# Holding the weight sums and low parts of every seven-product block in program order on VectorE

## The chip, the cores and the metric

The kernel runs on one core of one Trainium2 chip. A core has five engines that run side by side, each through its own instructions in order, and wait for one another through semaphores: TensorE (PE in the profile, its weight loads PEld), VectorE (DVE), ScalarE (ACT), GpSimd (POOL) and SyncE (SP), which here issues the transfers of the weights. The metric is the time of one execution on the device in microseconds (us).

## The reference

One decoder layer on 256 positions of width 2048, in float32: a half-step SwiGLU feed-forward network (FFN) of width 5632, a mixer with two head groups that share one input projection (2048 by 5120) and one output projection (2048 by 2048), a second half-step FFN, and a last RMS norm.

```python
x = x + 0.5 * swiglu_ffn(rms_norm(x, g1), w_gate, w_up, w_down)
z = rms_norm(x, mix_norm) @ w_in               # lru_x, lru_gate, sc_b, sc_c, sc_x
y_lru = rg_lru(conv4(lru_x) + b, ...) * gelu(lru_gate)
y_sc = sc_b * conv3(sc_c * sc_x)
x = x + concat(rms_norm(y_lru), rms_norm(y_sc)) @ w_out
x = x + 0.5 * swiglu_ffn(rms_norm(x, g2), ...)
return rms_norm(x, final_norm)
# swiglu_ffn(x) = (silu(x @ w_gate) * (x @ w_up)) @ w_down
```

Nearly all the arithmetic is in the three matrix products of each FFN.

## The kernel before

**Units of weights.** Weights come in units of 512 by 512 numbers, 1 MB each, laid out as 128 partitions by 2048. A unit is loaded by SyncE into a `raw` buffer (`load`, L181). `parts_of` (L208) splits it: ScalarE rounds it into a high part `hi` in two halves (CAST, 128x1024), and VectorE subtracts (`lo = raw - hi`, 128x2048), so that the product keeps float32's precision. The rows of the data are split the same way. TensorE multiplies high by high, low data by high weights, and high data by low weights: for one block of 128 rows that is 8 matmuls on `hi` and then 4 on `lo`, each 128x512. There are two buffers for a pair `hi`, `lo` (`splits`), and inside an FFN and the second half of the output projection a third (`split_tiles`, L194, every third unit). Three `raw` buffers turn, and two more, of tag "kept", hold the units that a block adds up.

**Seven-product blocks.** `seven` (L411) multiplies two row blocks by a two-by-two square of weight units with seven products in place of eight (Strassen's scheme in Winograd's form), and adds the remaining two units of the inner dimension in the usual way (`usual`). I call the eleven steps of a block, in program order: p0 (unit w11), p4 (sum A = w12 - w11), x (unit b2, both row blocks), p5 (sum B = w22 - w11), x (b3), p6 (sum C = w22 - w12), p2 (w22), x (a2), p3 (sum D = w21 - w11), x (a3), p1 (w21). A p-step is 12 matmuls, an x-step 24. The four sums are VectorE instructions in place in the raw buffers of w11 and w12 (`raw<-raw,raw` in the profile); their casts and low parts follow. ScalarE copies finished products out of PSUM (`snap`: s1 and s5 after p0 and p4, u2 after p5, u3 after p6), and a callback adds them up: `done(1, 1)` after p6 takes u3, s5 and bank e; `done(0, 1)` after p2 takes bank c and u2; `done(1, 0)` after the last x takes bank a; `done(0, 0)` after p1 takes bank d and s1.

**Where the blocks stand.** Each FFN has a first stage of single products, then five pairs of blocks, `gate` and `up` (callbacks at L876 and L881): a gate block adds four times on VectorE and applies Silu on ScalarE; an up block adds and multiplies (eight small VectorE instructions) and its results are transposed on TensorE into `h` and split again (`settle`, L549). After pairs 0, 2 and 4 comes `down` (L790): an ordinary product for columns 0, a seven-product block (`d`) for columns 1 and 2, an ordinary product for columns 3. The mixer has one such block in the input projection (`sc_c`, L1139, tiles `in_c`) and one in the output projection (`o_q`, with callbacks `own` and `done`, L1286 to L1290). That makes 28 blocks: 20 gate and up, 6 down, 2 in the mixer.

**What sets the order.** Every instruction is recorded through a thin class `Engine` (all have line L43), and a list scheduler then places each engine's instructions by its own estimate of times, except those that are pinned. `keep_in_program_order` pins an instruction behind the instruction recorded just before it on the same engine. Before, `sp.held` pins the loads up to the first gate block, and the opening stage of the first FFN is pinned whole up to the middle of its first gate block; VectorE's work in the other blocks is free.

Of the kernel before, what the change touches and what calls it, by code (L numbers as in the profile page):

```python
# [13 lines left out]
ALU = mybir.AluOpType  # L14
# [35 lines left out]
def hybrid_block(ctx: ExitStack, tc: tile.TileContext, a: dict, out: bass.AP):  # L50
    nc = tc.nc
    Engine.pinned = False
    dve, act, pe, sp = (Engine(tc, e) for e in (nc.vector, nc.scalar, nc.tensor, nc.sync))
# [25 lines left out]
    bigs = ctx.enter_context(tc.tile_pool(name="bigs", bufs=10, side="left"))  # L79
# [92 lines left out]
    def big(name):  # L172

        return bigs.tile([P, UK, 2 * S], F32R, tag="big", name=name)
# [3 lines left out]
    extra = []  # L178
    turn_of = {"split": 0}

    def load(src, name, pieces=((0, UK),), loaded=None, kept=False):  # L181
        if kept and extra:
            raw = extra[0].tile([P, UK, CW], F32, tag="kept", name=f"raw_{name}", bufs=2)
        elif kept:
            raw = bigs.tile([P, UK, CW], F32, tag="big", name=f"raw_{name}")
        else:
            raw = raws.tile([P, UK, CW], F32, tag="raw", name=f"raw_{name}")
        for i, e in pieces:
            sp.dma_start(raw[:, i:e, :], src[i * P : e * P].rearrange("(j p) c -> p j c", p=P))
            if loaded:  # L190
                loaded(i)
        return raw

    def split_tiles(name):  # L194
        pool, bufs = splits, 2
        if extra:
            turn_of["split"] += 1
            if turn_of["split"] % 3 == 0:
                pool, bufs = extra[0], 1
        return [pool.tile([P, UK, CW], F32R, tag=part, name=f"{part}_{name}", bufs=bufs) for part in ("hi", "lo")]  # L200

# [209 lines left out]
    def seven(w, rows, cols, sf, xs, name, keep, done, between=None, early=False, own=None, factor=None):  # L411

        apart = {}
        if own:
            a, c = (bank(f"ps_{name}_{n}") for n in "ac")
            apart.update({(t, 1): bank(f"ps_{name}_x{t}1") for t in range(NT)})  # L420
            d, e = bank(f"ps_{name}_d"), None
            apart.update({(t, 0): bank(f"ps_{name}_x{t}0") for t in range(NT)})
        else:
            a, c, e, d = (bank(f"ps_{name}_{n}") for n in "aced")

        def get(u, n, kept=False):
            src = w[u * UK * P : (u + 1) * UK * P, cols[n] : cols[n] + CW]
            return load(src, f"{name}_{u}{n}", kept=kept)

        (r0, r1), two = rows, len(xs) > 1  # L430
        w11, w12 = get(r0, 0, True), get(r0, 1, True)
        b2, w22 = get(xs[0][0], 1), get(r1, 1)
        b3 = get(xs[1][0], 1) if two else None
        a2, w21 = get(xs[0][0], 0), get(r1, 0)
        a3 = get(xs[1][0], 0) if two else None

        def snap(ps, n):
            s = keep(f"{n}_{name}")
            if factor:
                act.activation(s, ps, AF.Copy, scale=factor[n])  # L440
            else:
                act.copy(s, ps)
            return s

        def product_of(i, raw, ps, begin=False, end=True, blk=None):
            multiply([(ps, sf[i], begin, end)], blk or parts_of(raw, f"{name}_p{i}"), True)

        def usual(i, raw, n, *targets, first=None):

            blk = first or parts_of(raw, f"{name}_x{i}{n}")  # L450
            if own:
                last = i == len(xs) - 1
                targets = [(apart[t, n], t, i == 0, last) for t in range(NT)]
            multiply([(ps, stationary(xs[i][1], t), b, z) for ps, t, b, z in targets], blk, True)
            if own and last:
                for t in range(NT):
                    own(t, n, apart[t, n])

        product_of(0, w11, a, True)
        dve.tensor_tensor(w11, w12, w11, op=ALU.subtract)  # L460
        if early:
            between("first sum")
        product_of(4, w11, c, True)
        blk = None
        if early:
            between("second product")
            hi, lo = split_tiles(f"{name}_x01")
            act.copy(hi, b2)
            s1 = snap(a, "s1")
            dve.tensor_tensor(w11, w22, w11, op=ALU.subtract)  # L470
            low_part(b2, hi, lo)
            blk = blocks(hi, lo)
        else:
            s1 = snap(a, "s1")
        s5 = snap(c, "s5")
        if between:
            between(0)
        usual(0, b2, 1, (e, 1, True, not two), (c, 0, False, False), first=blk)
        if between:
            between(1)  # L480
        if not early:
            dve.tensor_tensor(w11, w22, w11, op=ALU.subtract)
        if between:
            between("sum")
        product_of(5, w11, a)
        blk = blk2 = None
        if early:
            blk = parts_of(b3, f"{name}_x11")
            hi2, lo2 = split_tiles(f"{name}_p2")
            act.copy(hi2, w22)  # L490
            blk2 = blocks(hi2, lo2)
        u2 = snap(a, "u2")
        if between:
            between(2)
        if two:
            usual(1, b3, 1, (e, 1, False, True), (c, 0, False, False), first=blk)
        if early:
            between("third sum")
        dve.tensor_tensor(w12, w22, w12, op=ALU.subtract)
        if early:  # L500
            low_part(w22, hi2, lo2)
            between("third low")
        product_of(6, w12, a)
        u3 = snap(a, "u3")
        if early:
            between("fifth product")
        done(1, 1, e, [u3, s5])
        product_of(2, w22, c, blk=blk2)
        done(0, 1, c, [u2])
        usual(0, a2, 0, (d, 0, True, False), (a, 1, False, False))  # L510
        dve.tensor_tensor(w11, w21, w11, op=ALU.subtract)
        product_of(3, w11, a, end=own is not None or not two)
        if early:
            between("sixth product")
        if two:
            usual(1, a3, 0, (a, 1, False, True), (d, 0, False, False))
        done(1, 0, a, [])
        product_of(1, w21, d, own is not None)
        done(0, 0, d, [s1])

    def ffn(tag, norm, after, opening=False):
        with tc.tile_pool(name=f"ffn{tag}", bufs=1, side="left") as fp:
# [26 lines left out]
            def settle():  # L549
                while waiting:  # L550
                    turn_hidden(*waiting.pop(0))
# [88 lines left out]
            ps = {(m, t): bank(f"ps_{m}{tag}_0_{t}") for m in "gu" for t in range(NT)}  # L640
# [223 lines left out]
            for s in range(5):  # L864
                cs = (CW + 2 * s * CW, 2 * CW + 2 * s * CW)
# [21 lines left out]
                def meanwhile(i):  # L887
# [23 lines left out]
                sp.held = False  # L911
                seven(
                    wu, (0, 1), cs, sf, xs, f"u{tag}_{s}", keep, up,
                    (lambda i: settle() if i == 1 else None) if opening and s == 0 else None,
                )
                if s % 2 == 0:
                    down(s == 4)
# [49 lines left out]
    with tc.tile_pool(name="mixer", bufs=1, side="left") as mp, tc.tile_pool(name="mixw", bufs=2, side="left") as mw:  # L967
# [168 lines left out]
            last()  # L1136
            part(2)

        def sc_c():  # L1139
            r2 = work.tile([P, NT], F32, tag="r2", name="r2")  # L1140
            dve.tensor_tensor(r2, nm.r, nm.r, op=ALU.mult)
            rt = [r2[:, t : t + 1] for t in range(NT)]
# [18 lines left out]
            def done(t, n, ps, tiles):  # L1161
# [10 lines left out]
                    turn(1)  # L1172

            c0 = 3 * (D // 2)
            seven(
                w_in, (0, 1), (c0 + CW, c0), si, [(u, nm.xT[u]) for u in (2, 3)], "in_c", lambda name: free.pop(0), done,
                factor={"s1": rt[0], "s5": rt[1], "u2": rt[0], "u3": rt[1]},
            )
            return lambda: turn(0)

        def sc_x(ps, half):
# [24 lines left out]
        behind = None  # L1206
        for i, (use, part, half) in enumerate(order):
            ps = columns(w_in, part * (D // 2) + half * CW, nm.xT, f"in_{part}_{half}", behind)
            behind = None
            if i == 0:  # L1210
                flush()
                nm.factor()
                nm.diagonals()
                nm.rows()
                bc = nm.bc
                use(ps, half)
                behind = sc_c()
                gate_weights("a", a["lru_w_a"][0])
                gate_weights("i", a["lru_w_i"][0])
                yT += [big(f"yT_{u}") for u in range(KD // UK)]  # L1220
            else:
                use(ps, half)
# [11 lines left out]
        for g in range(2):  # L1234
            if g == 1:
                flush()
            ps = product(w_out, 0, (2 * g, 2 * g + 1), yT.__getitem__, f"o0_{g}")
# [11 lines left out]
    with tc.tile_pool(name="outs", bufs=1, side="left") as op:  # L1249
# [36 lines left out]
        def done(t, n, ps, tiles):  # L1286
            add(2 - n, t, 0, *([] if ps is None else [ps]), *tiles)
            added(2 - n)
# [10 lines left out]

    fss = const.tile([P, NT, NC_D], F32, name="fss")  # L1300
    ov = out.rearrange("(t p) d -> p t d", p=P)

    def last(c, t):
        if c == 0 and t == 0:
# [10 lines left out]
            return work.tile([P, 1], F32, tag=tag, name=f"{tag}_{t}")  # L1315


        dve.scalar_tensor_tensor(xr, xr, -0.5, fin[:, cs], op0=ALU.mult, op1=ALU.mult)
        if c == NC_D - 2:
            pre = held[t] = single("pre")  # L1320
            dve.reduce_sum(pre, fss[:, t, : c + 1], axis=AX.X)
# [71 lines left out]
```

## Time and profile before

| what | value |
|---|---|
| median of 3 runs (lowest to highest) | 1729.67 us (1729.08 to 1730.92) |
| profiled execution, its own time | 1729.74 us |
| its span in the profile | 1728.0 us |
| TensorE busy | 1716.6 us, 99% |
| VectorE busy | 1509.8 us, 87% |
| ScalarE busy | 1077.7 us, 62% |
| granted TensorE clock | 0.999 |

The span is the time from the program's first to its last profiled instruction; 1.74 us of the execution's time lie around it. A busy TensorE is not a TensorE at its peak, since matmuls overlap: what counts is the distance from one matmul's start to the next's. In the rows of the timeline a group of equal instructions is one line, with its start, the time it covers, and in square brackets the idle time before it and who ended that.

### The profile page before, as it was taken

Reading aid. Unit: us, or ns where it says so; the run is one execution under the profiler, and the core shown is the slowest. Engines: PE = TensorE matmul, PEld = TensorE weight load, DVE = VectorE, ACT = ScalarE, POOL = GpSimd, SP = SyncE. Lnnn points to the kernel's source line nnn. Section 1 sums busy time; section 2 is a strip of 40 time slices with the busy share of each in tenths; the row PEclk is TensorE's granted clock in tenths of the full one; section 3 lists DMA queues with packets and bytes.
Section 4 is the critical chain, followed back from the end, with each engine's and each line's share of the span. In section 5 each row is a group of like instructions: output and inputs, shape, how many; then the busy total and the mean of one; then the engine's idle time right before and its main releaser. Section 6 shows DMA issues by size and latency. Waiting matters only on the chain.

```text
span 1728.0 us, 20332 instructions
## 1 busy us (share of the span) xinstructions
PE 1716.6 (99%) x7985; PEld 1433.5 (83%) x7985; DVE 1509.8 (87%) x1239; ACT 1077.7 (62%) x1406; POOL 7.0 (0%) x34
## 2 busy tenths in 40 slices
PE   9999999999999999999999999999999999999998
PEld 8888888888888888878888888888888888888886
DVE  7998989899789898787897989889899887899896
ACT  7666566656466666667966657656556664656654
POOL 0100000000000000000000000000000000000000
PEclk9999999999999999999999999999999999999999
DMA  8564565666466556555566574675665646555743
GB/s 300 191 237 141 208 228 186 206 230 219 156 211 204 202 178 219 171 169 197 172 195 203 188 243 144 199 240 187 212 210 195 218 147 219 195 195 195 257 156 122
DMA packets 174223, 343.22 MB, mean 199 GB/s; under 512 B 5684, under 2 KB 8624, under 8 KB 174000
## 3 DMA queue, kind: packets, MB, share of 16 engines
q1 hardware_dynamic: 173632, 340.81, 58.5%
q8 instruction: 62, 1.02, 0.2%
q10 hardware_dynamic: 176, 1.06, 0.2%
q14 instruction: 33, 0.27, 0.0%
q0 software_dynamic: 320, 0.07, 0.0%
HBM read 339.82 MB, written 2.10 MB: 198 GB/s over the span
## 4 chain that ended last, share of the span: by engine, by line
PE 97%; DVE 1%; DMA 1%; issue 0%; ACT 0%; DVEq 0%; ACTq 0%
PE ps_d L43 13%; PE ps_in L43 10%; PE ps_u_a L43 9%; PE ps_g_a L43 9%; PE ps_g_c L43 6%; PE ps_u_c L43 6%; PE ps_d_a L43 5%; PE ps_u_d L43 5%; PE ps_g_d L43 4%; PE ps_u_e L43 3%; PE ps_d_c L43 3%; PE ps_g_e L43 3%; PE ps_g L43 3%; PE ps_o L43 3%; PE ps_u L43 3%; PE ps_d_d L43 3%
## 5 line engine op out<-in xcount | busy, mean ns | idle before, releaser
L43 ACT CAST hi_g_p<-raw_g 128x1024 fp32r<-128x1024 f32 (+1 forms) x139 | 142.6, 1057 | 102.9 <-DVE raw_g L43 32.6
L43 DVE TENSOR_TENSOR lo_g_p<-raw_g,hi_g_p 128x2048 fp32r<-128x2048 f32 x70 | 159.7, 2287 | 32.0 <-ACT hi_g_p L43 31.8
L43 ACT CAST hi_u_p<-raw_u 128x1024 fp32r<-128x1024 f32 x140 | 141.4, 1050 | 67.6 <-DVE raw_u L43 24.7
L43 DVE TENSOR_TENSOR lo_u_p<-raw_u,hi_u_p 128x2048 fp32r<-128x2048 f32 x70 | 159.2, 2286 | 19.7 <-ACT hi_u_p L43 19.4
L43 PE MATMUL ps_d<-hi_d,h 128*128 128x512 f32 x696 | 166.1, 390 | 0.0
L43 PEld LDWEIGHTS ps_d<-hi_d,h 128*128 128x128 f32 x696 | 130.0, 188 | 26.7
L43 ACT CAST hi_d<-raw_d 128x1024 fp32r<-128x1024 f32 x88 | 88.6, 1048 | 71.6 <-PE ps_u_d L43 17.4
L43 DVE TENSOR_TENSOR lo_d<-raw_d,hi_d 128x2048 fp32r<-128x2048 f32 x44 | 100.6, 2290 | 31.8 <-ACT hi_d L43 31.8
L43 PE MATMUL ps_in<-xT_nm,hi_in 128*128 128x512 f32 x512 | 122.5, 391 | 0.0
L43 ACT CAST hi_d_p<-raw_d 128x1024 fp32r<-128x1024 f32 x84 | 85.1, 1050 | 59.3 <-DVE raw_d L43 40.2
L43 PEld LDWEIGHTS ps_in<-xT_nm,hi_in 128*128 128x128 f32 x512 | 94.0, 188 | 18.9 <-ACT tha L43 0.5
L43 ACT CAST hi_g_x<-raw_g 128x1024 fp32r<-128x1024 f32 (+1 forms) x79 | 81.5, 1059 | 41.7 <-PE ps_g_c L43 24.6
L43 ACT CAST hi_u_x<-raw_u 128x1024 fp32r<-128x1024 f32 x80 | 80.4, 1046 | 38.7 <-PE ps_u_c L43 22.1
L43 DVE TENSOR_TENSOR lo_d_p<-raw_d,hi_d_p 128x2048 fp32r<-128x2048 f32 x42 | 95.6, 2287 | 7.9 <-ACT hi_d_p L43 7.7
L43 DVE TENSOR_TENSOR raw_u<-raw_u,raw_u 128x2048 f32<-128x2048 f32 x40 | 91.6, 2290 | 10.9 <-DMA raw_u<-in_ffn_w_up_dram 10.2
L43 DVE TENSOR_TENSOR lo_g_x<-raw_g,hi_g_x 128x2048 fp32r<-128x2048 f32 x40 | 91.4, 2286 | 7.7 <-ACT hi_g_x L43 7.6
L43 DVE TENSOR_TENSOR lo_in<-raw_in,hi_in 128x2048 fp32r<-128x2048 f32 x32 | 73.3, 2289 | 25.3 <-ACT hi_in L43 25.2
L43 DVE TENSOR_TENSOR raw_g<-raw_g,raw_g 128x2048 f32<-128x2048 f32 x40 | 91.5, 2288 | 4.2 <-DMA raw_g<-in_ffn_w_gate_dram 3.7
L43 DVE TENSOR_TENSOR lo_u_x<-raw_u,hi_u_x 128x2048 fp32r<-128x2048 f32 x40 | 91.4, 2285 | 0.2 <-ACT hi_u_x L43 0.2
L43 PE MATMUL ps_d<-lo_d,h 128*128 128x512 f32 x348 | 86.2, 389 | 0.0
L43 ACT CAST hi_in<-raw_in 128x1024 fp32r<-128x1024 f32 x64 | 63.9, 1044 | 25.4 <-PE ps_in L43 13.8
L43 PEld LDWEIGHTS ps_d<-lo_d,h 128*128 128x128 f32 x348 | 65.3, 188 | 13.6
(471 smaller groups left out, 3740.9 us busy)
## 6 DMA issues: line engine op xcount, KB each, us to landing
raw_d<-in_ffn_w_down_dram SPq DMA_DIRECT2D x88, 1024.0 KB, 5.1
raw_u<-in_ffn_w_up_dram SPq DMA_DIRECT2D x87, 1024.0 KB, 5.3
raw_g<-in_ffn_w_gate_dram SPq DMA_DIRECT2D x86, 1024.0 KB, 5.3
raw_in<-in_w_in_dram SPq DMA_DIRECT2D x32, 1024.0 KB, 5.1
raw_in_c<-in_w_in_dram SPq DMA_DIRECT2D x8, 1024.0 KB, 5.1
raw_o<-in_w_out_dram SPq DMA_DIRECT2D x8, 1024.0 KB, 5.1
raw_o_q<-in_w_out_dram SPq DMA_DIRECT2D x8, 1024.0 KB, 5.1
xres<-in_x_dram SPq DMA_DIRECT2D x3, 512.0 KB, 10.0
```

The lines of the kernel that those rows point to most:

```text
L43: ins = getattr(self.engine, name)(*args, **kwargs)
```

## The change

There are three edits.

1. In `seven`, VectorE is held (`dve.held = True`) from the start of the block to its end. Each of its own instructions, the four sums and the low parts, is pinned behind the VectorE instruction recorded just before it. The callbacks `done`, `between` and `own` are wrapped by `aside`, which records what they issue unpinned.
2. The input projection's block gets a third pair of split buffers, taken from the pool `bigs` (`extra` holds that pool during the block), and the work of the first head group's columns, `use(ps, half)`, moves from ahead of the block to a place inside it, after its first x-step.
3. In the last FFN's final step, the multiplication of column 0 by the norm's gain is put in a list and recorded when the next columns come, not at once.

```diff
@@ load, split_tiles
-        if kept and extra:
+        if kept and extra[0] is not bigs:
...
             if turn_of["split"] % 3 == 0:
+                if extra[0] is bigs:
+                    return [big(f"{part}_{name}") for part in ("hi", "lo")]
                 pool, bufs = extra[0], 1
@@ seven
+        def aside(fn):
+            def call(*args):
+                dve.held = False
+                fn(*args)
+                dve.held = True
+
+            return fn and call
+
+        done, between, own = aside(done), aside(between), aside(own)
+        dve.held = True
...
         done(0, 0, d, [s1])
+        dve.held = False
@@ sc_c
-        def sc_c():
+        def sc_c(between):
...
+            extra.append(bigs)
             seven(
                 w_in, (0, 1), (c0 + CW, c0), si, [(u, nm.xT[u]) for u in (2, 3)], "in_c", lambda name: free.pop(0), done,
+                lambda i: between() if i == 1 else None,
                 factor={"s1": rt[0], "s5": rt[1], "u2": rt[0], "u3": rt[1]},
             )
+            extra.clear()
...
-                use(ps, half)
-                behind = sc_c()
+                behind = sc_c(lambda: use(ps, half))
@@ last
+    gains = []
...
-        dve.scalar_tensor_tensor(xr, xr, -0.5, fin[:, cs], op0=ALU.mult, op1=ALU.mult)
+        gains.append(lambda: dve.scalar_tensor_tensor(xr, xr, -0.5, fin[:, cs], op0=ALU.mult, op1=ALU.mult))
+        if c:
+            while gains:
+                gains.pop(0)()
```

## The prediction

> **What bounds the kernel now.** I read the page's busy rows, then the chain that ended last, then who TensorE waited for, then the stretches of single blocks, and last the timeline of one block.
>
> ```profile
> span 1728.0 us, 20332 instructions
> PE 1716.6 (99%) x7985; PEld 1433.5 (83%) x7985; DVE 1509.8 (87%) x1239; ACT 1077.7 (62%) x1406; POOL 7.0 (0%) x34
> PE 97%; DVE 1%; DMA 1%; issue 0%; ACT 0%; DVEq 0%; ACTq 0%
> ```
>
> ```profile
> PE idle L43 <- DVE ones L43: 1.1, 1, 1.1
> PE ps_in_c_c L43 <- ACT v_snap L43: 0.8, 1, 0.8
> PE ps_u_c L43 <- DVE lo_u_p L43: 0.8, 1, 0.8
> PE ps_d_a L43 <- DVE lo_d_p L43: 0.3, 1, 0.3
> PE ps_g L43 <- ACT hi_g L43: 0.2, 1, 0.2
> ```
>
> TensorE is the chain, and it waited 3.2 us in all (five waits, the last column their length). So the time can hardly fall: the three waits inside seven-product blocks (0.8, 0.8, 0.3) sum to 1.9 us. VectorE at 87% has little room, and the next rows (stretches: length, then busy time by engine) show how little it is inside blocks: a gate and up pair, an up block alone, the block `o_q`, the block `in_c`, a short and a long `d` block.
>
> ```profile
> core 0: us, PE busy (x) PEld busy (x) DVE busy (x) ACT busy (x) POOL busy (x), PEclk, DMA share, GB/s
> 201.44:283.96 82.52, 82.52 (x370) 68.40 (x369) 72.68 (x42) 49.33 (x58) 0.00 (x0) 1.00 0.61 204
> 1245.70:1286.50 40.80, 40.80 (x182) 33.80 (x181) 37.77 (x21) 25.48 (x29) 0.00 (x0) 1.00 0.61 207
> 982.05:1022.85 40.80, 40.80 (x181) 33.80 (x181) 35.15 (x23) 25.01 (x33) 0.00 (x0) 1.00 0.55 180
> 730.53:773.72 43.19, 42.41 (x190) 34.30 (x189) 39.46 (x38) 29.47 (x41) 0.30 (x3) 1.00 0.45 143
> 155.08:185.10 30.02, 30.02 (x134) 24.70 (x133) 29.10 (x23) 19.26 (x24) 0.00 (x0) 1.00 0.48 168
> 390.32:431.36 41.04, 41.04 (x181) 33.97 (x182) 36.99 (x42) 25.21 (x30) 0.00 (x0) 1.00 0.70 231
> ```
>
> In the pair VectorE is free for 82.52 - 72.68 = 9.8 us, 4.9 a block, and TensorE never waits. Blocks keep up because the scheduler lets VectorE run ahead: it puts sum C next to A, long before C's use, fills the time in which a sum's casts run on ScalarE with other low parts, and puts the adds of finished products behind the next low part. VectorE's timeline of that gate block shows it.
>
> ```profile
> 194.18 4.71 DVE L43 TENSOR_TENSOR raw_g<-raw_g,raw_g 128x2048 f32<-128x2048 f32 x2
> ...
> 201.01 1.28 DVE L43 SCALAR_TENSOR_TENSOR xres<-ps_d,xres 128x512 f32<-128x512 f32 x2
> ...
> 204.40 2.28 DVE L43 TENSOR_TENSOR raw_g<-raw_g,raw_g 128x2048 f32<-128x2048 f32 x1
> 209.43 2.29 DVE L43 TENSOR_TENSOR lo_g_p<-raw_g,hi_g_p 128x2048 fp32r<-128x2048 f32 x1 [2.74 <-ACT hi_g_p L43]
> 211.64 2.29 DVE L43 TENSOR_TENSOR lo_g_x<-raw_g,hi_g_x 128x2048 fp32r<-128x2048 f32 x1
> 213.84 2.29 DVE L43 TENSOR_TENSOR lo_g_p<-raw_g,hi_g_p 128x2048 fp32r<-128x2048 f32 x1
> ...
> 223.94 0.69 DVE L43 TENSOR_TENSOR u_g<-u_g,s_g 128x512 f32<-128x512 f32 x1 [0.28 <-ACT u_g L43]
> 224.67 0.69 DVE L43 TENSOR_TENSOR u_g<-ps_g_e,u_g 128x512 f32<-128x512 f32 x1
> 225.28 2.28 DVE L43 TENSOR_TENSOR lo_g_p<-raw_g,hi_g_p 128x2048 fp32r<-128x2048 f32 x1
> 227.48 0.68 DVE L43 TENSOR_TENSOR u_g<-ps_g_c,u_g 128x512 f32<-128x512 f32 x1
> ...
> 237.62 4.62 DVE L43 TENSOR_TENSOR raw_u<-raw_u,raw_u 128x2048 f32<-128x2048 f32 x2
> ```
>
> A and C run as one group of two (194.18; the next block's at 237.62). Sum B at 204.40 is followed by its own low part at 209.43, and there VectorE sits idle for 2.74 us.
>
> **The change, part by part.** *Edit 1.* The order of the built instructions shows VectorE in a gate block as: low p0, A, low p4, low x, B, low p5, low x, C, low p6, add (u3, s5), add (bank e), low p2, add (bank c), low x, D, low p3, low x, low p1, add (bank d); then the next block's low p0. Two things follow. All four sums stand directly before their own low part. And the adds, though recorded unpinned, are in effect pinned too: the next low part is pinned behind the instruction recorded just before it, and that is the callback's last add. So low p2 queues behind u3's add, which needs p6 finished and copied; low x behind bank c's add, which needs p2 finished; the next block's low p0 behind bank d's add, which needs p1 finished. VectorE's lead over TensorE is gone three times a block. TensorE's own order interleaves the next step's `hi` matmuls where it expects to wait, which hides part.
>
> The prices, from ScalarE's and TensorE's timelines, and one transfer:
>
> ```profile
> 240.00 2.00 ACT L43 CAST hi_u_p<-raw_u 128x1024 fp32r<-128x1024 f32 x2 [0.74 <-DVE raw_u L43]
> 206.92 0.59 ACT L43 COPY s_g<-ps_g_c 128x512 f32<-128x512 f32 x1 [2.13 <-PE ps_g_c L43]
> ```
>
> ```profile
> 212.16 1.98 PE L43 MATMUL ps_g_a<-hi_g_p,xs 128*128 128x512 f32 x8
> 213.97 1.07 PE L43 MATMUL ps_g_a<-lo_g_p,xs 128*128 128x512 f32 x4
> 214.88 1.98 PE L43 MATMUL ps_g_e<-hi_g_x,x 128*128 128x512 f32 x8
> ```
>
> ```profile
> raw_g<-in_ffn_w_gate_dram SPq DMA_DIRECT2D x86, 1024.0 KB, 5.3
> ```
>
> A low part or sum costs 2.29 us, 2.20 behind another (211.64 to 213.84). From a sum's end to its low part: 0.1 us to the cast, 2.00 for both halves, 0.02 more: 2.12. A small add costs 0.69; a second costs 0.60 if it is independent (201.01: two in 1.28) and 0.73 if it uses the first's result (223.94 to 224.67). Four `lo` matmuls end 1.07 us after the first starts; one matmul follows another after (214.88 - 212.16) / 12 = 0.227 us.
>
> One gate block, walked along VectorE from the end of the previous block's last add: low p0 2.29; A 2.20; casts 2.12; lows p4 and x and sum B 2.29 + 2.20 + 2.20 (13.3 so far); casts 2.12; lows p5, x and sum C 6.69 (22.1); casts 2.12; low p6 2.29 (26.5). Then p6 on TensorE and u3's copy, 1.07 + 0.59 + 0.09 = 1.75; two adds 1.42; low p2 2.20 (31.9); p2's last matmuls 1.11; add 0.69; low x 2.20; D 2.20 (38.1). Before D's casts ScalarE has those of the last x in its order, whose unit is loaded into w22's buffer, free when low p2 ends: 31.9 + 5.3 + 0.1 + 2.0 = 39.3, so D's casts end at 41.3; low p3 2.29 (43.6). From there TensorE has 32 matmuls to the end of p1, 31 x 0.227 + 0.39 = 7.4, in which the two remaining lows (4.4) are hidden; add 0.69. End: 51.7 us, against 40.8 now: +10.9. Nothing on this chain may overlap, since each step waits for the one before; TensorE's 40.8 us of work fit beside it.
>
> An up block has three more multiplications on the chain (behind bank e's, bank c's and bank d's adds, 0.73 each), and takes 82.52 - 40.80 = 41.7 now: 51.7 + 2.2 = 53.9, +12.2. Twenty gate and up blocks less the first FFN's opening gate, which is pinned by hand up to its middle already: 9 x 10.9 + 10 x 12.2 = 220. Five of these blocks have two `h` low parts put ahead of B (0.60 each, one behind another): +6. The opening gate's second half: p6's adds ahead of its last x, +3, an estimate by the 1.42 and 1.75 above.
>
> `o_q` is the gate walk with the `own` adds of both x-banks queued ahead of C (bank complete and two adds: 4.3 later) and, with bank a's, ahead of low p1 (+1.9): 57.9 against 40.8, +17. The `d` blocks have no add that waits for u3 ahead of low p2. A short one: 13 sums and lows 28.7, four waits 8.5, six adds 3.9, less low p0 and A, done before it begins (4.5), less what falls into the waits (1.9): 34.7 against 30.0. A long one: 15 x 2.2 = 33.0, waits 8.5, adds 5.0, TensorE's end of 7.4 less two lows 3.0, less 2.7 of the next product's `hi` that is interleaved: 46.8 against 41.0. Together 2 x 4.7 + 4 x 5.8 = 33.
>
> *Edit 2*, first its rows:
>
> ```profile
> 727.00 4.62 DVE L43 TENSOR_TENSOR raw_in_c<-raw_in_c,raw_in_c 128x2048 f32<-128x2048 f32 x2
> 734.53 2.28 DVE L43 TENSOR_TENSOR lo_in_c_p<-raw_in_c,hi_in_c_p 128x2048 fp32r<-128x2048 f32 x1
> ```
>
> With the third pair of buffers, and C and the first columns' work moved from before low p4 to behind low x, low p4 ends near 733.7 (A's end, 727.0 + 2.29, + 2.12 + 2.29) and no longer at 736.8, so the 0.8 us wait on `ps_in_c_c` goes. Later the same pins hold. The walk, with the block's start as now: low p5 745.6, low p6 754.4, low p2 760.2, low p3 770.8, and 7.2 to p1's end: 778.0, not 773.7: +4.3. *Edit 3* moves two 0.69 us operations of the last `d` block; TensorE's chain there is set by lows, and I put it at nothing; if uncovered it costs 1.4. The removed waits give back 1.9.
>
> The sum: 220 + 6 + 3 + 17 + 33 + 4.3 - 1.9 = 281. The profiled execution is 1729.7 (span 1728.0 and 1.7 around it), the median the same within 0.1: 1729.7 + 281 = 2011 us.
>
> For the unknown I bound from both sides: ScalarE's casts may be earlier than their order suggests (below: the waits for casts fully hidden but for the adds, 3 us a block), or an x-cast that waits for its split buffer stands before C's casts (above: about 2.6 us in gate blocks, 20 to 30 in all). I take the walk as it is, since its every term is a row.
>
> **The rivals.** *Waits at the adds only.* If VectorE's idle 4.9 us a block absorb the casts, TensorE loses just what the adds cost it: after p6 it has 12 `hi` matmuls (0.91 + 2.72 us from low p6's end) while low p2 needs 1.75 + 1.42 + 2.20 = 5.37, a hole of 1.7; at the block's end add, low p0 and 0.16 against 1.81 of `hi` work, 1.2. Near 3 us x 20 + 10 = 1800. Against it: four waits of 2.12 are 8.5, more than 4.9.
>
> *TensorE's clock falls.* Behind low p2 TensorE has four matmuls (0.9 us) while the next low x is 1.11 + 0.69 + 2.20 = 4.0 away: a hole of 3.1 us in each block. If the granted clock fell to half for the eight `lo` matmuls that follow each, they would take 3.6 us and not 1.8: +36 over 20 blocks, 2047. The rows show 1.00 in every stretch, but no hole above 1.1 us. The Trainium skill (TensorE: Matmul & The Clock Gate, "HAM oscillation — how this bites in real kernels") says that idle gaps over some 3.4 us drop the array to half clock; no run here shows it, and the walk's largest gap lies just under.
>
> *Not slower.* The place is the same order of sums: late sums free VectorE for low parts needed sooner, TensorE's interleaved `hi` matmuls cover 2 us at each sum, and the price is a gain of the 1.9 us above: 1728. It decides if `hi` work of the next step (3.63 us in an x-step) is always ready and longer than what low p2 and low p0 lack; the 5.37 against 3.63 above says no.
>
> **How the numbers follow.** The walk 0.78, the adds only 0.12, the clock or a longer ScalarE queue 0.07, not slower 0.03. The likeliest gives 2011. The range from 1880 (half of the sums' waits hidden) to 2080 (the upper bound, with part of a clock loss) leaves out the rivals. Under 0.2% (3.5 us) a measurement tells nothing: slower 0.97, same 0.025, faster 0.005.
>
> **What would show it.** After: TensorE's waits for `lo_g_p`, `lo_u_p` and `lo_*_x` of VectorE in the hundreds of us, the chain with large shares of DVE and ACT; VectorE's waits for `hi_*_p` four a block, near 2.1 us each; an add of u_g or u_u that waits for ScalarE's copy ahead of a low part; the pair of blocks near 105 us, not 82.5. Wrong if the pair is under 90, that is if low p2's row follows p6 with no idle time before the adds.

## The result and the profile after

The changed kernel takes 2091.09 us (median of 5 runs, 2089.22 to 2091.95) against 1730.1 us before (median of 5, beside it). The ratio is 1.2087, with a 95% interval of 1.2071 to 1.2103: a loss of 361 us where 281 was forecast, 11 us beyond the upper end of the range. The profiled execution is the one of 2089.22 us.

First the page of the changed kernel: the span, the busy time of the engines, and the granted clock of TensorE in 40 slices (tenths, where before all were 9).

```profile
span 2087.4 us, 20189 instructions
PE 1862.0 (89%) x7985; PEld 1484.7 (71%) x7985; DVE 1521.0 (73%) x1239; ACT 1082.2 (52%) x1406; POOL 11.1 (1%) x34
PEclk9999999999999999999999898999988899988899
```

The same 7985 matmuls and 1239 VectorE instructions are there, VectorE's busy time is 11 us longer, and its share falls from 87% to 73%. TensorE's busy time grows by 145 us though it has no more work: a first sign of a slower clock. Its idle time grows by 214 us (from 11.4 to 225.4). Next, who waited for whom, from the view of waits (sum in us, number, longest):

```profile
DVE lo_u_p L43 <- ACT hi_u_p L43: 90.5, 40, 5.7
DVE lo_g_p L43 <- ACT hi_g_p L43: 86.1, 38, 4.8
DVE s_g L43 <- PE ps_g_d L43: 36.8, 10, 4.8
DVE h L43 <- ACT h L43: 28.7, 8, 8.3
DVE u_g L43 <- ACT u_g L43: 25.9, 10, 3.9
PE ps_g_d L43 <- DVE lo_g_x L43: 25.5, 9, 3.0
PE ps_u_c L43 <- ACT hi_u_p L43: 22.2, 10, 2.3
```

VectorE now waits four times a gate or up block for the casts behind a sum (78 waits, 177 us), for ScalarE's copy `u3` ahead of the adds, and for TensorE's last matmul at the block's end. TensorE in turn waits for VectorE's low parts (107 us for the blocks' low parts `lo_g_p`, `lo_u_p` and `lo_*_x`, 217 us of waits in all), which is the low end of the hundreds that were forecast. The forecast's sign on the chain cannot be read: the chain of the page breaks off (PE 6%, DVE 1%, the rest 0%). The stretches of a gate block, the up block behind it, gate block 2 of the second FFN, and the blocks `o_q` and `in_c` (40.8, 41.7, 41.7, 40.8 and 43.3 us before):

```profile
222.08:277.20 55.12, 46.74 (x181) 35.99 (x180) 36.23 (x19) 24.16 (x28) 0.00 (x0) 0.91 0.42 137
277.20:331.82 54.62, 47.20 (x190) 37.20 (x189) 39.52 (x24) 26.41 (x30) 0.00 (x0) 0.91 0.47 153
1555.35:1616.57 61.22, 49.93 (x189) 38.81 (x188) 38.31 (x22) 26.23 (x31) 0.00 (x0) 0.86 0.38 124
1139.43:1205.73 66.30, 48.22 (x181) 36.48 (x179) 45.87 (x31) 26.27 (x35) 0.00 (x0) 0.85 0.31 100
878.10:931.06 52.96, 44.20 (x191) 33.45 (x190) 41.61 (x39) 27.72 (x40) 0.30 (x3) 1.00 0.36 116
```

A stretch runs from the block's first matmul to the first one behind it. The pair is 109.7 us long, not 82.5 (105 was forecast), and every one of these stretches but the last has a granted clock below 1. VectorE's timeline of the first of them shows the forecast's walk:

```profile
225.20 2.29 DVE L43 TENSOR_TENSOR raw_g<-raw_g,raw_g 128x2048 f32<-128x2048 f32 x1
229.55 2.29 DVE L43 TENSOR_TENSOR lo_g_p<-raw_g,hi_g_p 128x2048 fp32r<-128x2048 f32 x1 [2.06 <-ACT hi_g_p L43]
...
238.32 2.29 DVE L43 TENSOR_TENSOR lo_g_p<-raw_g,hi_g_p 128x2048 fp32r<-128x2048 f32 x1 [2.07 <-ACT hi_g_p L43]
...
249.79 2.29 DVE L43 TENSOR_TENSOR lo_g_p<-raw_g,hi_g_p 128x2048 fp32r<-128x2048 f32 x1 [4.78 <-ACT hi_g_p L43]
254.04 0.69 DVE L43 TENSOR_TENSOR u_g<-u_g,s_g 128x512 f32<-128x512 f32 x1 [1.95 <-ACT u_g L43]
...
259.01 0.69 DVE L43 TENSOR_TENSOR u_g<-ps_g_c,u_g 128x512 f32<-128x512 f32 x1 [1.29 <-PE ps_g_c L43]
...
267.01 2.29 DVE L43 TENSOR_TENSOR lo_g_p<-raw_g,hi_g_p 128x2048 fp32r<-128x2048 f32 x1 [2.90 <-ACT hi_g_p L43]
...
277.40 0.69 DVE L43 TENSOR_TENSOR s_g<-ps_g_d,s_g 128x512 f32<-128x512 f32 x1 [3.70 <-PE ps_g_d L43]
```

Each of the four sums is followed by an idle VectorE until its casts are done, and the adds are waited for in the three places named. Two waits are longer than the walk had them: C's (4.78 against 2.12) and the one at the end (3.70 against 3.0). The granted clock has to do with both: at full clock, in the second run of experiment 5, they are 3.14 and 3.22. Stretches of 3.41 us of the same block, with TensorE's busy time and the granted clock:

```profile
222.72:226.14 3.42, 2.25 (x10) 1.42 (x8) 3.38 (x3) 0.00 (x0) 0.00 (x0) 1.00 0.00 0
226.14:229.55 3.41, 1.22 (x6) 0.80 (x5) 1.35 (x1) 2.58 (x3) 0.00 (x0) 1.00 0.00 0
229.55:232.97 3.42, 3.42 (x10) 2.63 (x9) 3.42 (x2) 0.00 (x0) 0.00 (x0) 0.50 0.00 0
...
256.86:260.27 3.41, 1.20 (x4) 0.67 (x4) 2.12 (x3) 0.53 (x1) 0.00 (x0) 1.00 0.34 77
260.27:263.68 3.41, 1.72 (x4) 1.44 (x5) 3.41 (x2) 0.69 (x2) 0.00 (x0) 0.50 0.76 249
```

A stretch in which TensorE is busy for 1.2 of 3.41 us is followed by one at half clock; 2.25 of 3.42 is not. The trace has 47 such drops, 262 us at half clock in all, against one of 7 us before, which lies behind the last matmul and costs nothing.

### The profile page after: what moved, and what is told of

Read it like the earlier page. It is cut to its first block, busy times and chain, and to the rows that moved or that the text cites. A ratio compares the mean times of both kernels' runs of the same rounds, so it can differ in the third digit from the quotient of the medians.

```text
span 2087.4 us, 20189 instructions
## 1 busy us (share of the span) xinstructions
PE 1862.0 (89%) x7985; PEld 1484.7 (71%) x7985; DVE 1521.0 (73%) x1239; ACT 1082.2 (52%) x1406; POOL 11.1 (1%) x34
## 5 line engine op out<-in xcount | busy, mean ns | idle before, releaser
L43 PE MATMUL ps_u_c<-hi_u_p,xs 128*128 128x512 f32 x160 | 58.9, 502 | 22.2 <-ACT hi_u_p L43 22.2
```

Source lines behind the costliest of these rows:

```text
L43: ins = getattr(self.engine, name)(*args, **kwargs)
```

## The experiments

Times are of single runs, except where a ratio is given, so differences of 2 or 3 us between them are not read.

**1. Without the hold.** Edits 2 and 3 stay.

```diff
-        done, between, own = aside(done), aside(between), aside(own)
-        dve.held = True
```

> VectorE is not held in the seven-product blocks; the third split buffer of the input projection, the moved column work and the deferred gain stay. Theory (the whole price is the hold): 1726 to 1731 us, TensorE's waits back under 5 us. Rival (the other two edits cost something of their own, by the moved column work or the buffers taken from the pool): 1735 us or more, with new waits in the input projection's block.

1736.1 us, 1.0033 of before (1.0020 to 1.0045). The rival holds for a small part: the hold, put on top of the two other edits, makes 355 of the 361 us, and those two alone cost 6. The block `in_c` is shorter (41.8 us against 43.3), so the loss lies elsewhere: behind `o_q`, which neither edit touches. That block's own matmuls take 40.8 us as before, but the first product of the stage behind it waits for a cast:

```profile
1027.67 6.73 PE L43 MATMUL ps_g<-hi_g,xT_n 128*128 128x512 f32 x16 [5.58 <-ACT hi_g L43]
```

**2. The counter put back.** `split_tiles` gives every third unit the extra pair. With the third pair in the input projection, its eleven units move that counter on by two, and in all later blocks other steps get the extra pair. This run, too, is without the hold.

```diff
             extra.append(bigs)
+            count = turn_of["split"]
...
             extra.clear()
+            turn_of["split"] = count
```

> No hold, and the counter by which every third pair of split buffers comes from the extra pool is put back after the input projection's block, whose eleven splits moved it on. Theory (the 5.7 us of the block o_q and 3.0 of the stage behind it without the hold are the counter's new phase, which gives other steps the third pair): o_q back to 40.8 us and 1727 to 1730 us in all, with the 1.5 us that the input projection's block gains. Rival (the buffers of the pool are what o_q and the next stage lack): 1734 to 1738.

1728.06 us (11 runs) against 1730.72 (15 runs): 0.9982, interval 0.9973 to 0.9991, faster than both kernels, by 0.2% against the one before. The stretch of `o_q` to the next stage's first matmul, first in experiment 1, then here:

```profile
981.13:1027.67 46.54, 40.96 (x181) 33.61 (x179) 38.08 (x28) 25.97 (x35) 0.00 (x0) 0.99 0.48 161
```

```profile
981.38:1022.18 40.80, 40.80 (x181) 33.78 (x180) 35.14 (x23) 25.22 (x33) 0.00 (x0) 1.00 0.55 181
```

So edits 2 and 3 together are worth 2 to 3 us, of which 1.5 stand in `in_c` (41.8 us against 43.3), and edit 2's side effect on the counter cost 8 (1736.1 - 1728.1). The same line in the held kernel:

> The changed kernel with only the counter of split buffers put back after the input projection's block. Theory (without the hold the counter cost 8 us; under the hold o_q's excess over the forecast is 8.4): 2079 to 2085 us, o_q near 58. Rival (under the hold the third pair no longer matters, since VectorE is late anyway): 2088 to 2094, o_q near 66.

2064.67 us: 26 less, more than the 8 expected. The stretch of `o_q` falls from 66.3 to 58.5, as the theory said. Of the 66.3, the last 4.4 were again the next stage's wait for a cast; where the 58.5 end, four matmuls of the block (0.9 us) are still to come. The rest is in the gate blocks 0, 2 and 4 of the second FFN, which fall from 61 to 64 us to some 56. Experiment 3 shows what these wait for.

**3. Sum B free of `h`.** The callback `settle` records the low parts of `h` between the first x-step and sum B, so B is pinned behind them.

```diff
+        def apart_of(fn):
+            def call(*args):
+                fn(*args)
+                dve.loose = True
+
+            return fn and call
...
-        done, between, own = aside(done), aside(between), aside(own)
+        done, between, own = aside(done), apart_of(aside(between)), aside(own)
```

After such a callback the next held instruction is pinned behind the last held one.

> The changed kernel, but sum B is pinned behind the low part before it and no longer behind the low parts of h, which the callback records between; the adds stay as they are. Theory (in the second FFN the transposes of the up block before stand behind the whole first x-step in TensorE's order, so sum B waits for TensorE): gate blocks 0, 2 and 4 of the second FFN fall from 61 to 64 us to 53 to 56, and the time to 2062 to 2075 us. Rival (the waits for h only stand in for waits that come anyway): 2083 to 2092.

2064.75 us, 26 less. Gate block 2 of the second FFN in the changed kernel, TensorE and then VectorE:

```profile
1569.64 0.60 PE L43 MATMUL ph<-ident,z 128*128 128x128 f32 x4
...
1574.01 0.60 PE L43 MATMUL ph<-ident,s_g 128*128 128x128 f32 x4
1579.34 3.78 PE L43 MATMUL ps_g_a<-hi_g_p,xs 128*128 128x512 f32 x8 [4.73 <-ACT hi_g_p L43]
```

```profile
1570.89 0.69 DVE L43 TENSOR_TENSOR h<-ph,h 128x512 fp32r<-128x512 f32 x1 [2.79 <-ACT h L43]
1575.26 0.69 DVE L43 TENSOR_TENSOR h<-ph,h 128x512 fp32r<-128x512 f32 x1 [3.68 <-ACT h L43]
1575.87 2.28 DVE L43 TENSOR_TENSOR raw_g<-raw_g,raw_g 128x2048 f32<-128x2048 f32 x1
```

The second transpose stands behind the x-step's matmuls in TensorE's order. Its copy, the low part of `h`, sum B, B's casts follow one by one, and TensorE is idle for 4.73 us and then at half clock (eight matmuls in 3.78 us, not 1.98). With B free, the same block is

```profile
1542.84:1599.60 56.76, 47.99 (x189) 37.06 (x188) 38.40 (x22) 25.92 (x31) 0.00 (x0) 0.88 0.41 136
```

With the counter put back the two transposes stand next to each other (1550.55 and 1550.99) and the block is as short: the two cures act on the same wait. That the counter's phase moves the transposes is seen; by which of the scheduler's estimates is not.

**4. ScalarE's casts in order.** C's wait of 4.78 us was the upper bound that the forecast had named: the cast of a later x-unit stands ahead of C's.

```diff
     def parts_of(raw, name):
...
+        act.held = "own" if dve.held else False
         for h in (slice(0, 2), slice(2, UK)):
             act.copy(hi[:, h, :], raw[:, h, :])
+        act.held = False
```

Here and in experiment 6, "own" pins an instruction behind the last one that was pinned on its engine, not the last one recorded.

> The changed kernel with ScalarE's casts of weights in the blocks in program order among themselves, so that C's casts stand ahead of those of p2 and of the next x-step. Theory (C's wait of 4.8 us, where 2.1 was forecast, is ScalarE's order): VectorE's wait ahead of low p6 falls to about 2.1 us, and the time by 2.6 us in some 20 to 26 blocks, to 2020 to 2045 us. Rival (the 80 us above the forecast are TensorE's half clock, 262 us of it): within 15 us of 2089.

2087.93 us: the rival's number, and my theory at that point fell. The waits for casts do shrink, to a longest of 2.2 us:

```profile
DVE lo_g_p L43 <- ACT hi_g_p L43: 78.8, 39, 2.2
DVE lo_u_p L43 <- ACT hi_u_p L43: 78.4, 41, 2.2
DVE h L43 <- ACT h L43: 38.3, 6, 7.3
```

That is 19 us less waiting in sum (157.2 against 176.6), of which next to nothing reaches the end. The gate block shown above does fall from 55.1 to 52.6 us, but the wait for `h` grows by 10 and comes to gate blocks 2 and 4 of the first FFN too (60.2 us for block 2, 55.7 in the changed kernel), and the time at half clock grows from 262 to 278 us. So a long C wait in a handful of blocks is not the missing 80 us; what it is worth by itself, this run does not show.

**5. The clock.** Extra matmuls with thrown-away results fill TensorE's two longest holes of a block.

```diff
+        def fill(i, blk, ps, n):
+            for k in range(n):
+                pe.matmul(ps, sf[i][k % UK][0], blk[k % UK][1], start=True, stop=True, skip_group_check=True)
...
-        product_of(0, w11, a, True)
+        blk0 = parts_of(w11, f"{name}_p0")
+        product_of(0, w11, a, True, blk=blk0)
+        fill(0, blk0, d, 6)
...
+        blk2 = blk2 or parts_of(w22, f"{name}_p2")
         product_of(2, w22, c, blk=blk2)
+        if e is not None:
+            fill(2, blk2, e, 8)
```

> The changed kernel with 6 extra matmuls after p0 and 8 after p2 in each block, into a bank that holds nothing at that time (d before its first product, e after its adds), in the places where TensorE's two longest waits stand. They add work and take no wait away. Theory (a stretch of 3.41 us in which TensorE is busy less than some 0.41 is followed by one at half clock; part of that lies on the chain): the half-clock time falls from 262 us to under 80, and the time to 2045 to 2075 us. Rival A (all 80 us by which matmuls are longer lie on the chain): 2000 to 2020. Rival B (VectorE sets the end of every block, the clock costs nothing): 2085 to 2095, with the clock restored. Rival C (the clock follows the length of a wait, or something else): half-clock time as before.

2070.53 us with 384 matmuls more, and 72 us of half clock in place of 262: within theory, and all three rivals are out. (In the six down blocks the adds of bank e come later, so there the extra matmuls overwrite it and those sums are not the reference's.) The down blocks, which have less slack, took 17 us longer in sum. So the next run left them out:

> The extra matmuls after p0 and p2 in the gate and up blocks alone (not in the opening one). In the first run with them these blocks were about 2.2 us shorter each, while the six down blocks, whose TensorE has less slack, were 20 us longer in sum. Theory (half clock costs some 45 us on the chain): 2035 to 2052 us. Rival (the extra work and the clock cancel out): 2065 to 2075.

2052.21 us, 39 less than the changed kernel with 266 matmuls more, and 78 us of half clock left: at the edge of what theory gave. The gate block shown above, now at full clock, and VectorE's two long waits in it:

```profile
218.64:271.41 52.77, 46.44 (x196) 35.33 (x194) 36.24 (x19) 24.06 (x28) 0.00 (x0) 1.00 0.42 139
```

```profile
244.71 2.29 DVE L43 TENSOR_TENSOR lo_g_p<-raw_g,hi_g_p 128x2048 fp32r<-128x2048 f32 x1 [3.14 <-ACT hi_g_p L43]
271.61 0.69 DVE L43 TENSOR_TENSOR s_g<-ps_g_d,s_g 128x512 f32<-128x512 f32 x1 [3.22 <-PE ps_g_d L43]
```

**6. Which pins cost: adds or sums.** First the adds free, with sums and low parts in order among themselves (`dve.held = "own"`):

> Sums and low parts stay in program order among themselves, but none stands behind the adds of the callbacks any more. Theory (one chain on VectorE of fifteen sums and low parts, four waits for casts and the adds' waits for TensorE, of which TensorE hides nothing): a gate block needs 15 x 2.2 + 4 x 2.12 = 41.5 us, or 44.1 with the longer wait of C, against 55.1 in the changed kernel and 40.8 before: 1745 to 1800 us. Rival A (the adds' places alone cost the time): back to 1728 to 1740. Rival B (the waits for casts alone cost the time): stays above 1950.

1839.83 us: between theory and rivals, above my 1800. A gate block and the up block behind it:

```profile
209.24:250.61 41.37, 41.36 (x182) 33.54 (x180) 34.28 (x19) 23.09 (x27) 0.00 (x0) 1.00 0.53 179
250.61:297.38 46.77, 43.45 (x189) 33.92 (x188) 37.80 (x24) 25.90 (x30) 0.00 (x0) 1.00 0.51 182
```

The gate block's 41.4 looks like the 41.5 of the expectation, but that is luck: TensorE was busy for all of it, so its own work set the length. Only five of the nine gate blocks are like it (41.1 to 42.5 us); the four that stand right behind an up block take 46.7 to 49.5. The up blocks take 45.0 to 46.9. For these I had let the adds fall into the waits for casts. They do not: the four waits stay empty in the rows, the eight adds and multiplications come on top, and 37.8 busy and 9.0 of waits for casts (worked out from that block's rows) make the 46.8.

Then the sums early, with the adds pinned as in the changed kernel:

```diff
             between("first sum")
+        else:
+            dve.tensor_tensor(w12, w22, w12, op=ALU.subtract)
         product_of(4, w11, c, True)
...
         s5 = snap(c, "s5")
+        if not early:
+            dve.tensor_tensor(w11, w22, w11, op=ALU.subtract)
...
-        if not early:
-            dve.tensor_tensor(w11, w22, w11, op=ALU.subtract)
...
             between("third sum")
-        dve.tensor_tensor(w12, w22, w12, op=ALU.subtract)
+            dve.tensor_tensor(w12, w22, w12, op=ALU.subtract)
...
         dve.tensor_tensor(w11, w21, w11, op=ALU.subtract)
+        blk3 = parts_of(a3, f"{name}_x10") if two else None
...
-            usual(1, a3, 0, (a, 1, False, True), (d, 0, False, False))
+            usual(1, a3, 0, (a, 1, False, True), (d, 0, False, False), first=blk3)
```

> The hold stays, adds included, but the program order is changed: sum C stands right behind sum A, sum B ahead of the low part of the first x-step, and the low part of the last x-step ahead of that of p3, so that another low part lies between each sum and its own. Theory: the four waits for casts (4 x 2.12, and 2.6 more at C) go, the adds' places stay: a gate block about 43 to 44 us, 1785 to 1830 us in all. Rival A (the adds' places alone cost the time): above 2000. Rival B (the waits for casts alone cost it): 1728 to 1745.

1992.39 us, near rival A: the adds' places are by far the dearer pins. VectorE's wait for `u3`, now, and the gate block:

```profile
DVE u_u L43 <- ACT u_u L43: 68.1, 10, 6.9
```

```profile
220.25:271.75 51.50, 45.39 (x181) 35.70 (x180) 36.24 (x19) 23.84 (x28) 0.00 (x0) 0.93 0.46 158
```

What VectorE saves at the casts it spends waiting for p6 (6.9 us a block). TensorE itself needs 96 x 0.227 = 21.8 us from p0 to the end of p6, and it has two holes at the block's start (1.17 and 2.20 us here), which in the changed kernel are

```profile
225.22 1.21 PE L43 MATMUL ps_g_a<-lo_g_p,x 128*128 128x512 f32 x4 [1.17 <-DVE lo_g_p L43]
228.62 1.30 PE L43 MATMUL ps_g_c<-hi_g_p,xs 128*128 128x512 f32 x4 [2.19 <-ACT hi_g_p L43]
```

Together that is 25.2 us, against the 27.6 (26.5 + 1.07) at which the walk, casts and all, had p6 finished; in this run, with half clock behind the holes, p6 ends 28.4 us after the block's start. I had shortened VectorE's chain and forgotten that TensorE's is almost as long. Half clock is then paid on it:

> The held kernel with the sums early (1992 us, 196 us of half clock, where 1785 to 1830 had been expected), with the extra matmuls in gate and up blocks. Theory (once the sums are early TensorE's own 96 matmuls to the end of p6 set the chain, and half clock is paid there in full): 1940 to 1965 us, the half clock under 60 us. Rival (the adds' places alone make the 262 us): 1980 to 1995.

1938.82 us with 36 us of half clock left, just under the range: of the 262 us that the adds' places alone had cost (1992.4 against 1730), 54 were the clock. The gate block takes 48.8 at full clock, still 8.0 more than before, with 14 extra matmuls (3.2 us) in it.

Both cures together:

> Both cures at once: the sums stand early and no sum or low part stands behind an add, but sums and low parts stay in program order among themselves. Theory (the price is where sums and adds stand, and the two make up for each other's slack: 1840 with the adds free alone, 1992 with the sums early alone): 1730 to 1755 us. Rival (any fixed order of the low parts costs, since TensorE's needs differ from block to block): above 1780.

1768.0 us, 13 above the range. Of the 361 us, 323 are back: not the fixed order as such makes the loss, but the places that it gives to sums and adds. The order in these better places still costs 38 us. The gate blocks are mostly at 40.8 to 42, nine of the ten up blocks still take 43 to 46 us:

```profile
243.66:288.96 45.30, 42.70 (x189) 34.14 (x188) 39.29 (x25) 26.14 (x30) 0.00 (x0) 1.00 0.53 186
```

What the up blocks lack is left open; TensorE's longest waits inside blocks are for ScalarE there (12.1 us for the casts `hi_u_p`, 7.1 for the copy `s_u`). Above 1768 the two kinds of pins nearly add up: +224 for the adds, +72 for the sums, +323 for both.

**7. All three causes taken out.** The extra matmuls, B free of `h` and the counter put back, in the held kernel.

> The changed kernel with the extra matmuls in the gate and up blocks, sum B free of h's low parts, and the counter of split buffers put back: the three causes that the forecast lacked. Theory (what is left is the forecast's walk without its 6 for h: 1729.7 + 275 = 2005; by the single runs 2091 - 26 - 45 - 8 = 2012): 1998 to 2018 us. Rival (a fourth cause is in it, such as C's casts behind those of the next x-step): 2025 or more.

2018.41 us, at the upper edge of theory. A gate block, the next up block having 52.8, and `o_q`:

```profile
218.91:271.75 52.84, 46.47 (x196) 35.33 (x195) 36.24 (x19) 24.06 (x28) 0.00 (x0) 1.00 0.43 141
1120.09:1177.39 57.30, 45.55 (x177) 35.02 (x176) 41.10 (x27) 25.29 (x33) 0.00 (x0) 0.88 0.28 97
```

The walk gave 51.7 and 57.9; with the last four matmuls of `o_q`, which the stretch leaves out, it is 58.2. Summed over the profiled runs, each against before:

| blocks | forecast | changed kernel | experiment 7 |
|---|---|---|---|
| 9 gate blocks | +98, and 6 for `h` | +144 | +104 |
| 10 up blocks | +122 | +142 | +119 |
| `o_q` | +17 | +25.5 | +16.5 |
| `in_c` | +4.3 | +9.7 | +9.3 |
| all the rest | +34 | +38 | +41 |

## Why the prediction was right, and where it failed

The forecast had the cause and most of the size, and left out some 80 us: the clock was kept out of the sum, and the terms for `h` and for edit 2 were too small.

**Right: direction, mechanism, walk.** The loss is VectorE's fixed order. The walk's 220 us for gate and up blocks is 222 in experiment 7, `o_q` 58.2 for 57.9, and the waits are where the forecast put them. Some of that closeness is luck: gate blocks are above the walk and up blocks below it (+11.5 for 10.9 and +11.9 for 12.2 on average), with the extra matmuls in them. The down blocks' walk holds in its sum alone (+40 for 33 in the changed kernel): the short ones lost 7.0 and 10.9 where it had 4.7, the long ones 12.0, 1.8, 2.5 and 6.3 where it had 5.8. That the adds are in effect pinned too was the step that mattered most: with the adds free the loss is 110 us and not 361. Its weights were off, though. I treated casts and adds as equal parts of one chain, and the experiments give the adds two and a half to three times the price of the sums (224 and 72 us above 1768, or 251 and 99 below 2091).

**Failed: the rival on the clock, at 0.07.** "The rows show 1.00 in every stretch, but no hole above 1.1 us" was true of before and said nothing on a kernel with holes of 2 to 3 us. I took a single hole's length against the limit that I had read, and put the walk just under it. The fall of the clock costs at least 39 us here (2091.1 to 2052.2, with 78 us of half clock still there and 266 matmuls more). The mechanism is the one that the forecast gave that rival; that the size is near its 36 is luck, since the forecast had one drop a block, behind low p2, and the block shown above has a second at its start. It was no alternative to the walk but an addition to it, and should have stood in the sum.

**Failed: "two `h` low parts put ahead of B (0.60 each): +6".** I priced the two instructions and not what they wait for. They wait for ScalarE's copies of TensorE's transposes, which in the second FFN stand behind a whole x-step. In the place of 6 it is some 26 us.

**Failed: edit 2 at its own block only.** I followed the third pair of buffers in `in_c` and left out that the counter that hands it out goes on. In the changed kernel that is some 8 us in the stretch of `o_q`, and it is what puts the transposes so late. The counter and `h` together are 33.8 us (2052.2 to 2018.4).

**Failed: walks that end at the block's last matmul.** The stretch of `in_c` lost 9.7 and not 4.3. Its own last matmul comes 6.2 us later than before; the rest is a wait of the stage behind it, as with the 4.4 us behind `o_q`. No term held such a wait. Behind `o_q` it goes when the counter is put back (experiment 2); why the casts behind `in_c` come late was not tested.

```profile
931.06 3.94 PE L43 MATMUL ps_in<-xT_nm,hi_in 128*128 128x512 f32 x16 [3.46 <-ACT hi_in L43]
```

**The sum.** Experiment 7 is 289 us above before, where the walk without `h` gave 275; with 34 for `h` and the counter, and 39 for the clock, that makes the 361 measured; the 34 and the 39 are steps between single runs, in this order. The 14 us between 289 and 275 are not settled: experiment 7 still has 59 us of half clock, its extra matmuls, and C's wait at 3.15 us in the block shown where the walk had 2.12. The upper bound that I had named, an x-cast ahead of C's casts, exists (4.78 us in the changed kernel, 3.14 at full clock), but putting the casts in order gained nothing in all (experiment 4). The range's upper end was built on that and on a part of a clock loss, and had no room for `h` and the counter. Two smaller slips changed no term: the row at 1245.70, given as an up block alone, starts in the gate block before it; and half of the sums' waits, 4.2 us over 28 blocks, is 119 us, which puts the lower end at 1892 and not 1880.

**The other rivals.** "Waits at the adds only" at 1800 is nearest to the kernel of experiment 6 with the sums early: 1992, or 1939 with the holes filled. It put TensorE's holes at low p2 (1.7 us) and at the block's end (1.2). In the gate block shown there, TensorE does not wait for low p2; its longest waits are at the block's start (1.17 and 2.20 us) and for the low part of the x-step behind p2 (2.07). "Not slower" had nothing for it. Edit 3 was put at nothing, and in experiment 2 the last down block takes 41.1 us, 41.4 before.

## What to carry to other kernels

When an instruction is pinned behind another, price what that other one waits for, and on which engine, before its own duration: the term for `h` and the weight of the adds against the sums were both misjudged this way. Holes that a change puts into TensorE's work are to be summed over stretches of 3.41 us, since they can be paid for twice, as idle time and as half clock behind it. A walk along one block has to go on until the next stage's first product has its operands. And a counter or a rotation that a change touches in one block has to be followed through all later ones.

## What the hardware showed that was not expected

TensorE's clock fell behind holes far shorter than 3.4 us: in the changed kernel only 8 waits are longer than that, and there are 47 drops to half clock. The drops start on a grid of 3413 ns and last one to three of its stretches (3.41 to 10.24 us). In that trace every one follows a stretch in which matmuls, counted as 0.227 us for 512 columns and in proportion less for narrower ones, fill at most 0.38 of the time. Of the other stretches at full clock four fill 0.22 to 0.34, and each of these holds narrow matmuls, such as transposes; the rest fill 0.42 or more. Over the twelve runs of the experiments stretches of up to 0.41 were followed by a drop and some from 0.28 on were not, so the share counted in this way does not decide alone. The Trainium skill (TensorE: Matmul & The Clock Gate, "HAM oscillation — how this bites in real kernels") gives the rule as no idle gaps over some 3.4 us. These traces show that shorter gaps can be enough: in the block shown above, the stretch ahead of the first drop holds one hole of 2.19 us (the one of 1.17 lies in the stretch before). Extra matmuls with no use, 266 of them, made the kernel 39 us faster.
